# Gated MLP's up projection by Strassen's scheme over pairs of weight tiles

## The chip, the cores and the metric

One Trainium2 chip, one of its cores, one launch. The metric is the time of the program on the device in microseconds (us). The median of 3 runs of the kernel before is 1575.73 us (1575.71 to 1576.24).

The engines of a core have queues of their own and work them off in order: PE multiplies matrices, PEld is its weight load, DVE is the vector engine, ACT the scalar engine, POOL the GpSimd engine, and SP issues the transfers from memory. They wait for each other by semaphores.

## The reference

Two layers of a hybrid encoder, 512 tokens of 1024 columns, all in float32. A layer has attention with a short convolution beside it, merged and projected (`w_o`), then the gated MLP, then a gated embedding. What the change touches is the MLP:

```python
h = rmsnorm(x, g_ffn[i])                     # 512 x 1024
u = dwconv(h @ w_up[i], w_ffn_conv[i])       # 512 x 5632, three taps over the tokens
gate, value = jnp.split(u, 2, axis=-1)       # 2816 each
x = x + (silu(gate) * value) @ w_down[i]
```

(The four lines put the reference's MLP together in short form.)

## The kernel before

Every product is taken at near float32 precision from half-width parts: an operand is split into a high part, which ACT makes by a cast (`hh`, `wh`, `gth`), and a residue, which DVE makes by a subtraction (`hl`, `wl`, `gtl`). A product is then three matmuls, high by high, high by residue and residue by high (`mm3`, lines 88 to 90). Weights come by `weight`: a load of a 128x1024 tile on SP (L80), the cast on ACT (L83), the subtraction on DVE (L84). The ring of raw tiles holds 3, the rings of split tiles 5 each.

The MLP's up projection has 22 pairs of tiles, a gate tile and a value tile of 128 output columns each. A tile is 8 steps over the 1024 inputs, 3 matmuls each, with all 512 tokens as moving columns: 24 matmuls of 512 columns. Its sum lies in PSUM (`ps_mm` for gate tiles, `ps_sc` for value tiles). Then follow the three taps of the convolution (`taps`, L545 on ACT, L546 and L547 on DVE, read from PSUM), Silu of the gate tile (L572, ACT), the gated product (L574, DVE) and the split of the result (`gth`, `gtl`).

The down projection runs in three chunks, after 8, 16 and 22 pairs: for each half of the output columns and each of the four tiles of 128 tokens, `proj` sums the products of a chunk's pairs in PSUM (`ps_tp` in the first two chunks) and `residual` adds the sum to the stream `xs` (L525, DVE).

The MLP starts behind `w_o`, whose result goes through `residual` and `norm` tile of tokens by tile of tokens: Square with its sum on ACT (L117), the reciprocal root on POOL (L98, L99), scaling on DVE (L122, `ht`), transposes on PE (L125, `ps_tp`), split into `hh` and `hl`. While the last two tiles of tokens are normed, the first three up tiles (`NE = 3`, `ew`, `eo`) are multiplied in halves of 256 tokens. In the first half they need only tiles 0 and 1 of the tokens.

The order on each engine comes from a scheduler that places instructions when their inputs are ready and their buffers free; pools of buffers bind it. Where the change says so, PE's order is as written.

## Time and profile before

| | |
|---|---|
| median of 3 runs | 1575.73 us |
| span of the profiled execution | 1574.1 us |
| matmuls and transposes in the trace | 7288 |
| DVE instructions | 1228, 870.4 us busy |
| ACT instructions | 1088, 684.4 us busy |
| POOL instructions | 153, 103.0 us busy |
| transfers of `w_up` | 88 of 512 KB, 3.5 us from issue to landing |
| transfers of `w_down` | 44 of 512 KB, 3.4 us |

How lines are read: a row of the timeline has start, duration, engine, line, operation, output and inputs with their shapes; a bracket gives the idle time ahead of it and what ended it. A row of a group has the count, the busy time and mean duration in ns of one, and the idle time ahead. In the table of windows each engine has its busy time, and PEclk is the share of full clock granted.

### The profile page before, as it was taken

Reading aid. Unit: us, or ns where it says so; the run is one execution under the profiler, and the core shown is the slowest. Engines: PE = TensorE matmul, PEld = TensorE weight load, DVE = VectorE, ACT = ScalarE, POOL = GpSimd, SP = SyncE. Lnnn points to the kernel's source line nnn. Section 1 sums busy time; section 2 is a strip of 40 time slices with the busy share of each in tenths; the row PEclk is TensorE's granted clock in tenths of the full one; section 3 lists DMA queues with packets and bytes.
Section 4 is the critical chain, followed back from the end, with each engine's and each line's share of the span. In section 5 each row is a group of like instructions: output and inputs, shape, how many; then the busy total and the mean of one; then the engine's idle time right before and its main releaser. Section 6 shows DMA issues by size and latency. Waiting matters only on the chain.

```text
span 1574.1 us, 18521 instructions
## 1 busy us (share of the span) xinstructions
PE 1557.1 (99%) x7288; PEld 1280.1 (81%) x7288; DVE 870.4 (55%) x1228; ACT 684.4 (43%) x1088; POOL 103.0 (7%) x153
## 2 busy tenths in 40 slices
PE   7999999999999999999999999999999999999998
PEld 6888888888888888888888888888888888888886
DVE  7787553436544553555477775443565446535543
ACT  5678732325322431334464886222344234324342
POOL 2800000000000000001055000000000000000010
PEclk9999999999999999999999999999999999999999
DMA  6211122323213221323242102232232222232222
GB/s 205 93 55 41 54 94 94 106 69 129 95 61 130 93 95 58 132 96 94 71 133 81 41 28 92 81 107 81 85 118 94 94 94 94 80 107 94 94 68 79
DMA packets 41430, 142.06 MB, mean 90 GB/s; under 512 B 5761, under 2 KB 6273, under 8 KB 41345
## 3 DMA queue, kind: packets, MB, share of 16 engines
q1 hardware_dynamic: 41344, 140.90, 27.2%
q8 instruction: 57, 0.93, 0.2%
q14 instruction: 29, 0.23, 0.0%
HBM read 138.78 MB, written 2.10 MB: 90 GB/s over the span
## 4 chain that ended last, share of the span: by engine, by line
PE 94%; POOL 2%; DVE 2%; ACT 1%; DMA 1%; issue 1%; SPq 0%; DVEq 0%; POOLq 0%; ACTq 0%
PE ps_mm L89 14%; PE ps_mm L88 14%; PE ps_mm L90 14%; PE ps_sc L89 11%; PE ps_sc L88 11%; PE ps_sc L90 11%; PE ps_tp L89 4%; PE ps_tp L88 4%; PE ps_tp L90 4%; PE ps_tp L428 2%; PE ps_tp L125 1%; POOL rs L99 1%; PE ps_av L440 1%; PE ps_av L439 1%; PE ps_tp L394 1%; PE ps_av L88 1%
## 5 line engine op out<-in xcount | busy, mean ns | idle before, releaser
L84 DVE TENSOR_TENSOR wl<-raw,wh 128x1024 fp32r<-128x1024 f32 (+1 forms) x250 | 304.0, 1217 | 325.1 <-ACT wh L83 322.7
L83 ACT CAST wh<-raw 128x1024 fp32r<-128x1024 f32 (+1 forms) x250 | 260.8, 1046 | 425.6 <-PE ps_tp L90 120.3
L88 PE MATMUL ps_mm<-hh,wh 128*128 128x512 f32 (+1 forms) x832 | 326.4, 392 | 0.5 <-DVE ycv L355 0.5
L89 PE MATMUL ps_mm<-hl,wh 128*128 128x512 f32 (+1 forms) x832 | 322.9, 388 | 0.0
L90 PE MATMUL ps_mm<-hh,wl 128*128 128x512 f32 (+1 forms) x832 | 322.5, 388 | 0.0
L90 PEld LDWEIGHTS ps_mm<-hh,wl 128*128 128x128 f32 x832 | 156.6, 188 | 34.7
L88 PEld LDWEIGHTS ps_mm<-hh,wh 128*128 128x128 f32 x832 | 156.7, 188 | 33.2 <-DVE ycv L355 1.0
L89 PEld LDWEIGHTS ps_mm<-hl,wh 128*128 128x128 f32 x832 | 156.9, 189 | 32.5 <-DVE hl L94 0.4
L89 PE MATMUL ps_sc<-hl,wh 128*128 128x512 f32 (+1 forms) x368 | 142.2, 386 | 0.0
L90 PE MATMUL ps_sc<-hh,wl 128*128 128x512 f32 (+1 forms) x368 | 142.2, 386 | 0.0
L88 PE MATMUL ps_sc<-hh,wh 128*128 128x512 f32 (+1 forms) x368 | 142.1, 386 | 0.0
L98 POOL TENSOR_SCALAR ms<-ms 128x1 f32<-128x1 f32 (+2 forms) x40 | 15.8, 394 | 1389.0 <-ACT junk L117 1360.0
L89 PE MATMUL ps_tp<-wl,gth 128*128 128x512 f32 x256 | 100.6, 396 | 0.0
L90 PE MATMUL ps_tp<-wh,gtl 128*128 128x512 f32 x256 | 100.6, 395 | 0.0
L88 PE MATMUL ps_tp<-wh,gth 128*128 128x512 f32 x256 | 99.9, 395 | 0.0
L88 PEld LDWEIGHTS ps_sc<-hh,wh 128*128 128x128 f32 x368 | 69.3, 188 | 15.3
L90 PEld LDWEIGHTS ps_sc<-hh,wl 128*128 128x128 f32 x368 | 69.3, 188 | 15.3
L89 PEld LDWEIGHTS ps_sc<-hl,wh 128*128 128x128 f32 x368 | 69.3, 188 | 15.3
L93 ACT CAST gth<-fa 128x512 fp32r<-128x512 f32 x44 | 27.3, 620 | 120.1 <-DVE fa L574 120.1
L525 DVE TENSOR_TENSOR xs<-xs,ps_tp 128x512 f32<-128x512 f32 x32 | 21.6, 685 | 85.0 <-PE ps_tp L90 85.0
L572 ACT ACTIVATE fa<-fa 128x512 f32<-128x512 f32 x44 | 27.8, 632 | 88.5 <-DVE fa L547 88.5
L88 PEld LDWEIGHTS ps_tp<-wh,gth 128*128 128x128 f32 x256 | 48.1, 188 | 11.6
(242 smaller groups left out, 2671.2 us busy)
## 6 DMA issues: line engine op xcount, KB each, us to landing
raw<-in_w_up_dram SPq DMA_DIRECT2D x88, 512.0 KB, 3.5
raw<-in_w_down_dram SPq DMA_DIRECT2D x44, 512.0 KB, 3.4
raw<-in_w_g_dram SPq DMA_DIRECT2D x32, 512.0 KB, 3.5
raw<-in_w_z_dram SPq DMA_DIRECT2D x24, 512.0 KB, 3.5
raw<-in_w_o_dram SPq DMA_DIRECT2D x16, 512.0 KB, 3.5
raw<-in_w_pg_dram SPq DMA_DIRECT2D x16, 512.0 KB, 4.2
raw<-in_w_au_dram SPq DMA_DIRECT2D x8, 512.0 KB, 3.5
raw<-in_w_cu_dram SPq DMA_DIRECT2D x8, 512.0 KB, 3.5
```

The costliest lines, as they stand in the source:

```text
L83: nc.scalar.copy(h, raw)
L84: nc.vector.tensor_sub(lo, raw, h.bitcast(F32))
L88: nc.tensor.matmul(o, st[0], mv[0], start=start, stop=False)
L89: nc.tensor.matmul(o, st[0], mv[1], start=False, stop=False)
L90: nc.tensor.matmul(o, st[1], mv[0], start=False, stop=stop)
L93: nc.scalar.copy(hi, src)
L98: nc.gpsimd.tensor_scalar_add(ms, ms, EPS)
L99: nc.gpsimd.tensor_tensor(r, ms, negh[:, :n], ALU.pow)
L125: nc.tensor.transpose(tp[:, j * P:(j + 1) * P], ht[:, j * P:(j + 1) * P], ident)
L428: nc.tensor.transpose(tp[:, k * P:(k + 1) * P], pe[:, k * P:(k + 1) * P], ident)
L525: nc.vector.tensor_tensor(xs[:, t, c], xs[:, t, c], o, ALU.add)
L572: nc.scalar.activation(a, a, AF.Silu)
```

## The change

For 20 of the 22 pairs in each layer, the up projection is calculated by the Strassen scheme with Winograd's sums. A pair is a 2 by 2 problem: the inputs (1024) in two halves of 512, the two tiles of the pair as two halves of columns, and the tokens in two halves of 256. In place of 8 products of blocks it has 7, each of 4 steps by 3 matmuls with 256 moving columns: 84 matmuls of 256 columns in place of 48 of 512. The first two pairs (`NS = 2`) are four early tiles in halves of 256 tokens.

What comes with it:
- Sums of the quarters of h, once per layer on DVE (L581 to L586), split into `sh` and `sl`, and one quarter split again into `hh` and `hl`.
- Per pair four subtractions of 128x512 on POOL, in a chain on the raw weight tiles (`pair`, L614 to L617); three splits of 128x1024 and one of 128x512 (`vh`, `vl`) in place of two of 128x1024.
- Per pair three additions of 256 columns on DVE (L633, L647, L650) and four copies on ACT, which put the four quarters of the result into `C`. The taps now read `C`.
- The down projection runs in chunks of 4 pairs (the last of 2), in pieces of 12 matmuls of 512 columns that stand between the products: `residual` runs 48 times per layer in place of 24. The products of two pairs alternate, in an order of PE that is written by hand (`manual_schedule`).
- The pool of weight buffers is opened per layer and closed ahead of the MLP, where another (`wq`, 4 raw and 8 split tiles) is opened. The ring of `gth` and `gtl` holds 8 instead of 16, and the norms behind the MLP take their scratch from `tmp`.

```diff
-CHUNKS = ((0, 8), (8, 16), (16, 22))
+NS = 2
+NQ = 5
+HS = S // 2
...
+    def rawtile(n=1024):
+        wp, nr, nw = wpool[-1]
+        return wp.tile([P, n], F32, tag="raw", name="raw", bufs=nr)
...
+    def load(src, n=1024):
+        raw = rawtile(n)
         nc.sync.dma_start(raw, src)
-        h = wp.tile([P, n], F32R, tag="wh", name="wh")
-        lo = wp.tile([P, n], F32R, tag="wl", name="wl")
+        return raw
+
+    def wsplit(raw, n=1024, tag="w"):
+        wp, nr, nw = wpool[-1]
+        h = wp.tile([P, n], F32R, tag=tag + "h", name=tag + "h", bufs=nw if tag == "w" else 2)
+        lo = wp.tile([P, n], F32R, tag=tag + "l", name=tag + "l", bufs=nw if tag == "w" else 2)
         nc.scalar.copy(h, raw)
         nc.vector.tensor_sub(lo, raw, h.bitcast(F32))
         return h, lo
...
+    def weight(src, n=1024):
+        return wsplit(load(src, n), n)
...
+        wp, close_wp = pool("wp", l)
+        wpool.append((wp, 3, 5))
...
+        wpool.pop()
+        close_wp()
+        wp, close_wp = pool("wq", l)
+        wpool.append((wp, 4, 8))
...
-        KTOT = NJ
-        NE = 3
-        ew = [weight(w_up[l, i]) for i in range(NE)]
-        eo = [psum("sc" if i % 2 else "mm") for i in range(NE)]
+        ew = [weight(w_up[l, i]) for i in range(2 * NS)]
+        eo = [psum("sc" if i % 2 else "mm") for i in range(2 * NS)]
         for hf in range(2):
             c = slice(hf * 256, hf * 256 + 256)
-            for i in range(NE):
+            for i in range(2 * NS):
                 ws(eo[i][:, c], ew[i], hT, KD, P, 0, c)
         g3 = load_gain(l, 2, ff)
-        for j0, j1 in CHUNKS:
...
-            proj((lambda k, c: gt[k // 2][0][:, k % 2, c], lambda k, c: gt[k // 2][1][:, k % 2, c]),
-                 range(j0, j1), w_down[l], after_d, ("mm", "sc") if j1 == NJ else ("tp",))
+        quarter = [(slice(None), slice(2 * r, 2 * r + 2), slice(4 * k, 4 * k + 4), slice(None))
+                   for r in range(2) for k in range(2)]
+        hf = [ff.tile([P, 2, 4, P], F32, tag="gt", name="hf", bufs=8) for q in quarter]
+        V = nc.vector
+        for o, q in zip(hf, quarter):
+            V.tensor_tensor(o, hh[q].bitcast(F32), hl[q].bitcast(F32), ALU.add)
+        h11, h12, h21, h22 = hf
+        V.tensor_tensor(h22, h22, h21, ALU.add)
+        V.tensor_tensor(h21, h21, h11, ALU.subtract)
+        V.tensor_tensor(h11, h22, h11, ALU.subtract)
+        V.tensor_tensor(h12, h12, h11, ALU.subtract)
+        sh, sl = (ff.tile([P, 3, 2, 4, P], F32R, name=n) for n in ("sh", "sl"))
+        for i, src in enumerate((h22, h11, h12)):
+            split(sh[:, i], sl[:, i], src)
+        split(hh[quarter[2]], hl[quarter[2]], h21)
+
+        def quart(r, k0):
+            return lambda k: (hh[:, 2 * r:2 * r + 2, k0 + k, :], hl[:, 2 * r:2 * r + 2, k0 + k, :])
+
+        def summed(i):
+            return lambda k: (sh[:, i, :, k, :], sl[:, i, :, k, :])
+
+        gt = {}
+
+        def gated(j, u):
+            nc.scalar.activation(u[0], u[0], AF.Silu)
+            nc.vector.tensor_tensor(u[1], u[0], u[1], ALU.mult)
+            if j % 2 == 0:
+                gt[j // 2] = (ff.tile([P, 2, S], F32R, tag="gt", name="gth", bufs=8),
+                              ff.tile([P, 2, S], F32R, tag="gt", name="gtl", bufs=8))
+            split(gt[j // 2][0][:, j % 2, :], gt[j // 2][1][:, j % 2, :], u[1])
+
+        def pair(j):
+            r0, r1 = load(w_up[l, 2 * j]), load(w_up[l, 2 * j + 1])
+            b11, b21, b12, b22 = r0[:, :512], r0[:, 512:], r1[:, :512], r1[:, 512:]
+            w0 = wsplit(r0)
+            w22 = wsplit(b22, 512, "v")
+            g = nc.gpsimd
+            g.tensor_tensor(b22, b12, b22, ALU.subtract)
+            g.tensor_tensor(b12, b12, b11, ALU.subtract)
+            g.tensor_tensor(b11, b11, b22, ALU.subtract)
+            g.tensor_tensor(b21, b21, b11, ALU.subtract)
+            yield
+
+            def product(o, w, off, mv, first):
+                for k in range(4):
+                    c = slice(off + k * P, off + k * P + P)
+                    mm3(o, (w[0][:, c], w[1][:, c]), mv(k), first and k == 0, k == 3, not first)
+
+            C = ff.tile([P, 2, S], F32, tag="C", name="C", bufs=2)
+            U = ff.tile([P, HS], F32, tag="U", name="U", bufs=2)
+            y = psum("av")[:, :HS]
+            product(y, w0, 512, quart(0, 4), True)
+            yield
+            x = psum("mm")[:, :HS]
+            product(x, w0, 0, quart(0, 0), True)
+            nc.scalar.copy(U, y)
+            V.tensor_tensor(C[:, 0, :HS], x, U, ALU.add)
+            w1 = wsplit(r1)
+            yield
+            z = psum("sc")[:, :HS]
+            product(z, w1, 0, summed(0), True)
+            w2 = wsplit(r0)
+            yield
+            product(x, w2, 0, summed(1), False)
+            U = ff.tile([P, HS], F32, tag="U", name="U", bufs=2)
+            Z = ff.tile([P, HS], F32, tag="U", name="Z", bufs=2)
+            nc.scalar.copy(U, x)
+            nc.scalar.copy(Z, z)
+            yield
+            product(x, w1, 512, quart(1, 0), False)
+            V.tensor_tensor(C[:, 1, HS:], x, Z, ALU.add)
+            yield
+            product(z, w22, 0, summed(2), False)
+            V.tensor_tensor(C[:, 1, :HS], z, U, ALU.add)
+            yield
+            product(x, w2, 512, quart(1, 4), False)
+            nc.scalar.copy(C[:, 0, HS:], x)
+            gated(j, [taps(2 * j + i, C[:, i, :]) for i in range(2)])
+
+        def down(j0, j1, after, tags):
+            nk = (j1 - j0) // 2
+
+            def tiles(n):
+                return [weight(w_down[l, n * (NJ // 2) + j0 // 2 + k]) for k in range(nk)]
+
+            wt = tiles(0)
+            for n in range(2):
+                for t in range(NT):
+                    yield
+                    tk = slice(t * P, (t + 1) * P)
+                    o = psum(tags[t % len(tags)])
+                    for i in range(2 * nk):
+                        h, lo = gt[j0 // 2 + i // 2]
+                        wh, wl = wt[i // 2]
+                        c = slice((i % 2) * 512, (i % 2) * 512 + 512)
+                        mm3(o, (h[:, i % 2, tk], lo[:, i % 2, tk]), (wh[:, c], wl[:, c]), i == 0, i == 2 * nk - 1)
+                    after(t, n, o)
+                    if n == 0 and t == 2:
+                        nxt = tiles(1)
+                if n == 0:
+                    wt = nxt
+
+        downs = []
+
+        def piece():
+            while downs and next(downs[0], downs) is downs:
+                downs.pop(0)
+
+        def advance(g, n=1):
+            for _ in range(n if g else 0):
+                next(g, None)
+
+        for j in range(NS):
+            gated(j, [taps(2 * j + i, eo[2 * j + i]) for i in range(2)])
+        region = tc.manual_schedule(engines={mybir.EngineType.PE})
+        region.__enter__()
+        old, new = None, pair(NS)
+        advance(new)
+        for q in range(NS, NJ + 1):
+            nxt = pair(q + 1) if q + 1 < NJ else None
+            advance(old)
+            advance(new)
+            piece()
+            advance(old)
+            advance(new, 2)
+            advance(nxt)
+            piece()
+            advance(old, 2)
+            if old and q % 4 == 0:
+                downs.append(down(q - 4, q, residual, ("tp",)))
+            old, new = new, nxt
+        for _ in range(8):
+            piece()
+        region.__exit__(None, None, None)
...
+        for _ in down(4 * NQ, NJ, after_d, ("mm", "sc")):
+            pass
...
-                norm(t, gn, ff)
+                norm(t, gn, None)
```

(Below `-  for j0, j1` the old loop over pairs is left out; it is the one described above.)

Three places in the order. First PE at the start of the MLP in layer 0. Before, from the eighth matmul of the first early tile on (`ps_mm_3316` is its sum; `ht_3223` and `ht_3232` the two halves of token tile 2):

```order
1519 L88 MATMUL ps_mm_3316<-hh_71,wh_3300 128x256
1520 L89 MATMUL ps_mm_3316<-hl_72,wh_3300 128x256
1521 L90 MATMUL ps_mm_3316<-hh_71,wl_3301 128x256
1522 L125 MATMUL ps_tp_3225<-ident_73,ht_3223 128x128 x4
1523 L125 MATMUL ps_tp_3234<-ident_73,ht_3232 128x128 x4
1524 L88 MATMUL ps_mm_3316<-hh_71,wh_3300 128x256
```

Now, from the last matmul of `w_o` (`ps_sc_3241`) on; `ht_3273` and `ht_3282` are token tile 3, `ps_mm_3326` is the first early tile:

```order
1512 L103 MATMUL ps_sc_3241<-wh_3087,me_2096 128x512
1513 L138 MATMUL ps_tp_3225<-ident_70,ht_3223 128x128 x4
1514 L138 MATMUL ps_tp_3234<-ident_70,ht_3232 128x128 x4
1515 L138 MATMUL ps_tp_3275<-ident_70,ht_3273 128x128 x4
1516 L138 MATMUL ps_tp_3284<-ident_70,ht_3282 128x128 x4
1517 L101 MATMUL ps_mm_3326<-hh_68,wh_3304 128x256
```

The transposes of token tiles 2 and 3 moved ahead of every matmul of the MLP; before, those of tile 2 stood 9 matmuls behind its start and those of tile 3 at row 1583, 70 rows behind.

Second, DVE at the same place. Before, weight splits (`wl`) stand between the norm's operations:

```order
357 L122 SCALAR_TENSOR_TENSOR ht_3223<-xs_70,rs1_3220,gbc_2937 128x512
358 L122 SCALAR_TENSOR_TENSOR ht_3232<-xs_70,rs1_3220,gbc_2937 128x512
359 L84 TENSOR_TENSOR wl_3307<-raw_3304,wh_3306 128x1024
360 L84 TENSOR_TENSOR wl_3313<-raw_3310,wh_3312 128x1024
361 L94 TENSOR_TENSOR hl_72<-ps_tp_3184,hh_71 128x512
362 L84 TENSOR_TENSOR wl_3487<-raw_3484,wh_3486 128x1024
363 L525 TENSOR_TENSOR xs_70<-xs_70,ps_sc_3241 128x512
```

Now, behind the scaling of token tile 3; `hf` are the quarter sums, `wl_3305`, `wl_3311`, `wl_3317` and `wl_3323` the four early tiles:

```order
364 L107 TENSOR_TENSOR hl_69<-ps_tp_3275,hh_68 128x512
365 L581 TENSOR_TENSOR hf_3524<-hh_68,hl_69 128x1024
366 L581 TENSOR_TENSOR hf_3525<-hh_68,hl_69 128x1024
367 L581 TENSOR_TENSOR hf_3526<-hh_68,hl_69 128x1024
368 L107 TENSOR_TENSOR hl_69<-ps_tp_3284,hh_68 128x512
369 L94 TENSOR_TENSOR wl_3305<-raw_3302,wh_3304 128x1024
370 L581 TENSOR_TENSOR hf_3527<-hh_68,hl_69 128x1024
371 L94 TENSOR_TENSOR wl_3311<-raw_3308,wh_3310 128x1024
372 L583 TENSOR_TENSOR hf_3527<-hf_3527,hf_3526 128x1024
373 L94 TENSOR_TENSOR wl_3317<-raw_3314,wh_3316 128x1024
374 L94 TENSOR_TENSOR wl_3323<-raw_3320,wh_3322 128x1024
```

The first weight split stands behind the norm of the last token tile and three sums of h.

Third, DVE at the first taps. Before, taps of the early tiles (`ps_mm_3316`, `ps_sc_3317`, `ps_mm_3318`) and a weight split stand in turn, and PE's next products write other sums:

```order
373 L84 TENSOR_TENSOR wl_3601<-raw_3598,wh_3600 128x1024
374 L547 SCALAR_TENSOR_TENSOR fa_3465<-ps_mm_3316,wfc_3296,fa_3465 128x511
375 L546 SCALAR_TENSOR_TENSOR fa_3470<-ps_sc_3317,wfc_3296,fa_3470 128x511
376 L84 TENSOR_TENSOR wl_3637<-raw_3634,wh_3636 128x1024
377 L546 SCALAR_TENSOR_TENSOR fa_3479<-ps_mm_3318,wfc_3296,fa_3479 128x511
```

Now, from the split of the fourth quarter of h on; `C_3590` is the result of pair 2, `ps_mm_3605` its sum x, `raw_3641` and `raw_3737` are tiles of pairs 3 and 4:

```order
393 L107 TENSOR_TENSOR hl_69<-hf_3526,hh_68 128x2x512
394 L565 SCALAR_TENSOR_TENSOR fa_3560<-ps_mm_3328,wfc_3300,fa_3560 128x511
395 L564 SCALAR_TENSOR_TENSOR fa_3564<-ps_sc_3329,wfc_3300,fa_3564 128x511
396 L602 TENSOR_TENSOR fa_3550<-fa_3546,fa_3550 128x512
397 L94 TENSOR_TENSOR wl_3734<-raw_3641,wh_3733 128x1024
398 L94 TENSOR_TENSOR wl_3742<-raw_3737,wh_3741 128x1024
399 L633 TENSOR_TENSOR C_3590<-ps_mm_3605,U_3591 128x256
```

The first C addition of pair 2, which must have read x before the next product is added onto it, stands behind most taps of the early tiles and the weight splits of the next pairs.

More of the change, by code (lines that the diff above doesn't have):

```diff
@@ L63, in encoder_kernel @@
     cp = ctx.enter_context(tc.tile_pool(name="cp", bufs=1))
[L64 removed]
+    wpool = []
     tmp = ctx.enter_context(tc.tile_pool(name="tmp", bufs=2))
@@ L85, in weight, with mm3 @@
         return h, lo
-    def mm3(o, st, mv, start, stop):
-        nc.tensor.matmul(o, st[0], mv[0], start=start, stop=False)
-        nc.tensor.matmul(o, st[0], mv[1], start=False, stop=False)
-        nc.tensor.matmul(o, st[1], mv[0], start=False, stop=stop)
+    def weight(src, n=1024):
+        return wsplit(load(src, n), n)
+    def mm3(o, st, mv, start, stop, more=False):
+        nc.tensor.matmul(o, st[0], mv[0], start=start, stop=False, skip_group_check=more)
+        nc.tensor.matmul(o, st[0], mv[1], start=False, stop=False, skip_group_check=more)
+        nc.tensor.matmul(o, st[1], mv[0], start=False, stop=stop, skip_group_check=more)
     def split(hi, lo, src):
@@ L114, in norm @@
     def norm(t, g, pool):
-        junk = pool.tile([P, D], BF16, tag="junk", name="junk", bufs=1)
+        junk = pool.tile([P, D], BF16, tag="junk", name="junk", bufs=1) if pool else tmp.tile([P, D], BF16, tag="t2", name="junk", bufs=4)
         ms = sm.tile([P, 1], F32, tag="ms", name="ms")
@@ L120, in norm @@
             c = slice(half * 512, half * 512 + 512)
-            ht = pool.tile([P, 512], F32, tag="ht", name="ht", bufs=3)
+            ht = pool.tile([P, 512], F32, tag="ht", name="ht", bufs=3) if pool else tmp.tile([P, 512], F32, tag="t2", name="ht", bufs=4)
             nc.vector.scalar_tensor_tensor(ht, xs[:, t, c], r, g[:, c], ALU.mult, ALU.mult)
@@ L207, in layer @@
         for i in range(2):
-            raw = wp.tile([P, H * DQK], F32, tag="raw", name="raw", bufs=3)
-            nc.sync.dma_start(raw, w_uq[l, i])
+            raw = load(w_uq[l, i], H * DQK)
             w = tuple(lat_p.tile([P, H * DQK], F32R, name=f"wu{i}{n}") for n in "hl")
@@ L558, in layer @@
         g3 = load_gain(l, 2, ff)
-        for j0, j1 in CHUNKS:
-            gt = {}
-            for j in range(j0, j1):
-                av = []
-                for i in (2 * j, 2 * j + 1):
-                    if i < NE:
-                        o = eo[i]
-                    else:
-                        w = weight(w_up[l, i])
-                        o = psum("sc" if i % 2 else "mm")
-                        ws(o, w, hT, KD, P, 0)
-                    a = taps(i, o)
-                    if i % 2 == 0:
-                        nc.scalar.activation(a, a, AF.Silu)
-                    av.append(a)
-                nc.vector.tensor_tensor(av[1], av[0], av[1], ALU.mult)
-                if j % 2 == 0:
-                    gt[j // 2] = (ff.tile([P, 2, S], F32R, tag="gt", name="gth", bufs=16),
-                                  ff.tile([P, 2, S], F32R, tag="gt", name="gtl", bufs=16))
-                split(gt[j // 2][0][:, j % 2, :], gt[j // 2][1][:, j % 2, :], av[1])
-            def after_d(t, n, o, last=(j1 == NJ)):
-                residual(t, n, o)
-                if last and n == 1:
-                    norm(t, g3, ff)
-            proj((lambda k, c: gt[k // 2][0][:, k % 2, c], lambda k, c: gt[k // 2][1][:, k % 2, c]),
-                 range(j0, j1), w_down[l], after_d, ("mm", "sc") if j1 == NJ else ("tp",))
@@ L592, in layer, with after_d @@
+        for _ in range(8):
+            piece()
+        region.__exit__(None, None, None)
+        def after_d(t, n, o):
+            residual(t, n, o)
+            if n == 1:
+                norm(t, g3, None)
+        for _ in down(4 * NQ, NJ, after_d, ("mm", "sc")):
+            pass
+        ph = ff.tile([P, 2, S], F32R, tag="gt", name="ph", bufs=8)
+        pl = ff.tile([P, 2, S], F32R, tag="gt", name="pl", bufs=8)
+        raw = load(pT[l])
         split(ph, pl, raw.rearrange("p (k s) -> p k s", k=2))
-        pw = [ff.tile([P, D], F32, tag="gt", name="pw", bufs=16) for t in range(NT)]
+        pw = [ff.tile([P, D], F32, tag="gt", name="pw", bufs=8) for t in range(NT)]
@@ L618, in layer @@
         close_ff()
+        wpool.pop()
+        close_wp()
     for l in range(L):
```

7 lines of the change are left out of this document (removed).

## The prediction

> **What bounds the kernel now.** I read the page first: span, busy times and the chain that ended last; then the table of windows for one FF stage.
>
> ```profile
> span 1574.1 us, 18521 instructions
> PE 1557.1 (99%) x7288; PEld 1280.1 (81%) x7288; DVE 870.4 (55%) x1228; ACT 684.4 (43%) x1088; POOL 103.0 (7%) x153
> PE 94%; POOL 2%; DVE 2%; ACT 1%; DMA 1%; issue 1%; SPq 0%; DVEq 0%; POOLq 0%; ACTq 0%
> core 0: us, PE busy (x) PEld busy (x) DVE busy (x) ACT busy (x) POOL busy (x), PEclk, DMA share, GB/s
> 395.00:760.00 365.00, 365.00 (x1579) 294.07 (x1578) 188.10 (x223) 126.74 (x164) 4.17 (x8) 1.00 0.29 94
> ```
>
> The span is 1574.1 us, and 1.6 us lie around it: the median of the runs is 1575.73. PE is busy 99% and is 94% of the chain. Inside the FF stage of layer 0 it is busy all 365.00 us at full clock, while DVE has work for 188.10, ACT for 126.74 and POOL for 4.17. So only fewer or shorter matmuls can help, and whatever is added to DVE or POOL is free until it makes PE wait.
>
> **What is gained.** The price of a matmul is the distance between starts, not its printed length, since matmuls are pipelined.
>
> ```profile
> 559.76 0.40 PE L88 MATMUL ps_sc<-hh,wh 128*128 128x512 f32 x1
> 585.53 0.39 PE L90 MATMUL ps_sc<-hh,wl 128*128 128x512 f32 x1
> 372.29 0.28 PE L90 MATMUL ps_sc<-hh,wl 128*128 128x256 f32 x1
> 375.93 0.28 PE L90 MATMUL ps_mm<-hh,wl 128*128 128x256 f32 x1
> 372.29 0.19 PEld L88 LDWEIGHTS ps_sc<-hh,wh 128*128 128x128 f32 x1
> ```
>
> 110 steps of 512 columns take 25.77 us, 0.2343 each; 31 steps of 256 columns take 3.64, 0.1174 each. A weight load lasts 0.19, yet a 256-column stream runs at 0.117: loads overlap and do not bind. A pair cost 48 × 0.2343 = 11.25 us and now costs 84 × 0.1174 = 9.86. That is 1.38 less, and for 20 pairs in each of 2 layers **55.3 us**. The down products keep their number and width.
>
> **The steady lap.** One pair and two down pieces of 12 matmuls are a lap: PE needs 9.86 + 24 × 0.2343 = 15.48 us. There are 17 such laps in a layer (q = 5 to 21), 34 in all. DVE gets three C additions of 256 columns and a second residual addition; POOL, idle here before, gets four subtractions of 128x512.
>
> ```profile
> L84 DVE TENSOR_TENSOR wl<-raw,wh 128x1024 fp32r<-128x1024 f32 x242 | 295.9, 1224 | 324.3 <-ACT wh L83 322.1 <-PE ps_tp L394 0.5
> L547 DVE SCALAR_TENSOR_TENSOR fa<-ps_mm,wfc,fa 128x511 f32<-128x511 f32 x44 | 33.0, 749 | 1.4
> L94 DVE TENSOR_TENSOR gtl<-fa,gth 128x512 fp32r<-128x512 f32 x44 | 30.5, 692 | 28.8 <-ACT gth L93 28.8
> L94 DVE TENSOR_TENSOR lq_l<-ps_tp,lq_h 128x256 fp32r<-128x256 f32 x8 | 3.3, 416 | 0.4 <-ACT lq_h L93 0.4
> L83 ACT CAST wh<-raw 128x1024 fp32r<-128x1024 f32 x242 | 253.7, 1051 | 422.6 <-PE ps_tp L90 120.3 <-PE ps_mm L89 106.8 <-PE ps_sc L89 72.3
> 375.33 1.23 DVE L84 TENSOR_TENSOR wl<-raw,wh 128x1024 fp32r<-128x1024 f32 x1 [4.75 <-ACT wh L83]
> 376.47 0.74 DVE L546 SCALAR_TENSOR_TENSOR fa<-ps_mm,wfc,fa 128x511 f32<-128x511 f32 x1
> 377.13 1.22 DVE L84 TENSOR_TENSOR wl<-raw,wh 128x1024 fp32r<-128x1024 f32 x1
> ```
>
> With these rows DVE's lap is 4 weight splits (three of the pair, one of the down weights on average) 4.90, 4 taps 3.00, five operations of 512 columns (half split, gated product, its split, two residuals) 3.46 and three of 256 columns 1.25: 12.6 us. Queued operations start about 0.08 before the one ahead ends (376.47 against 375.33 + 1.23), which makes it 11.3. ACT has four casts of 1.05 and some smaller work, under 10 us, and does not bind.
>
> For POOL the trace has no 128x512 operation of this kind.
>
> ```profile
> 821.34 0.22 POOL L253 TENSOR_TENSOR kr<-ra,rb 128x16 f32<-128x16 f32 x1
> 82.34 0.46 POOL L253 TENSOR_TENSOR qc<-ra,rb 128x128 f32<-128x128 f32 x1
> L252 POOL TENSOR_TENSOR qc<-ra,rb 128x128 f32<-128x128 f32 x8 | 5.5, 688 | 10.1 <-DVE rb L251 10.1
> ```
>
> From 16 to 128 columns it grows by 0.24 us, 2.1 ns a column, so 512 columns give about 1.27; the bounds are 0.69 (DVE's duration for that shape) and 2.75 (four times the mean of 0.688). I take 1.27, the straight line through undisturbed rows: 5.1 us per lap.
>
> Does POOL slow DVE? These rows say it does.
>
> ```profile
> 78.40 0.69 DVE L332 TENSOR_TENSOR qc<-qc,rs 128x512 f32<-128x512 f32 x1 [2.87 <-POOL rs L99]
> 834.75 0.46 POOL L252 TENSOR_TENSOR qc<-ra,rb 128x128 f32<-128x128 f32 x1
> 834.81 0.94 DVE L332 TENSOR_TENSOR qc<-qc,rs 128x512 f32<-128x512 f32 x1 [0.18 <-POOL rs L99]
> 835.17 0.91 POOL L253 TENSOR_TENSOR qc<-ra,rb 128x128 f32<-128x128 f32 x1
> 819.53 1.23 DVE L84 TENSOR_TENSOR wl<-raw,wh 128x1024 fp32r<-128x1024 f32 x1
> 819.59 1.28 POOL L250 TENSOR_TENSOR ra<-krope,cg 128x32 f32<-128x32 f32 x1 [1.01 <-DVE krope L288]
> ```
>
> The DVE product of 0.69 lasts 0.94 when POOL started 0.06 earlier, and the next POOL operation lasts 0.91 for 0.46; a tiny POOL operation lasts 1.28 beside a weight split. Each seems to wait for the whole of the other. [...] Nothing overlapping, a lap is 11.3 + 5.1 = 16.4 us; with the DVE operations that read PSUM (the C and residual additions, 2.2 queued) hidden under POOL it is 14.2. PE's 15.48 lies between. So a lap loses from 0 to 0.92 us. I take 0.2, because DVE's queue has idle time that takes most POOL operations: 34 × 0.2 = **6.8 us**, with 0 and 31 as bounds. [...]
>
> **The start of each FF stage.** Here the order shows the loss.
>
> ```profile
> 333.25 28.30 SPq L80 DMA_DIRECT2D raw<-in_w_up_dram  x7
> 358.79 0.39 PE L90 MATMUL ps_sc<-wh,me 128*128 128x512 f32 x1
> 359.01 0.28 PE L88 MATMUL ps_mm<-hh,wh 128*128 128x256 f32 x1
> 361.12 0.68 DVE L525 TENSOR_TENSOR xs<-xs,ps_sc 128x512 f32<-128x512 f32 x1
> 362.83 1.05 ACT L117 ACTIVATE junk<-xs 128x1024 bf16<-128x1024 f32 x1
> 364.97 1.41 DVE L122 SCALAR_TENSOR_TENSOR ht<-xs,rs,gbc 128x512 f32<-128x512 f32 x2 [0.79 <-POOL rs L99]
> ```
>
> Before, FF matmuls follow the last w_o matmul without a gap (358.79, 359.01), on weights loaded from 333 on and split ahead; the norm of the last row tile (361.12 to 366.4, over 5 us) is covered. Call 359.0 T. Now all transposes of the norm stand ahead of the first FF matmul in PE's queue, so PE waits for that chain, to about T + 5. Behind it DVE's queue holds two residue splits and three quarter sums, then the first weight split: T + 5 + 2 × 0.6 + 3 × 1.14, and with the casts' waits T + 11.6. The three other weight splits alternate with sums of h, to T + 17. So the four early tiles, 192 matmuls of 0.1174 = 22.5 us, of which few can start ahead of the first split, end near T + 11.6 + 22.1 = T + 33.7 in place of T + 24.4 (22.5 and 1.9 of transposes): **9.3 us** lost. Loads 2 to 4, now issued only after w_o, land before their casts on ACT come up, so they add nothing. Next, pair 2's products y, x and z follow, 12 matmuls each, to T + 37.9; the product added onto x waits until the first C addition (L633) has read x, and this stands on DVE behind the taps of three early tiles and the weight splits of the next pairs, whose casts wait for six POOL operations in series: T + 41.7 to 44.4, so **3.8 to 6.5** more. A product of a later pair (z, whose weight goes through POOL, cast and split) waits about 1.6. Sum 14.7 to 17.4; I take **17 per layer, 34 us**, near the upper end since POOL's chain and DVE's sums lie in the same stretch. With POOL at 0.69 per operation it is 12, with every operation waiting for another over 20.
>
> **The layer boundary.** Opening the weight pool anew per layer lets the w_a loads of layer 1 start only when w_pg's tiles are free.
>
> ```profile
> 781.87 0.33 SPq L80 DMA_DIRECT2D raw<-in_w_a_dram  x1
> raw<-in_w_a_dram SPq DMA_DIRECT2D x8, 416.0 KB, 4.0
> ```
>
> Before, the last of the four loads was issued at 781.87, under w_pg. Now it follows the first split: 4.0 for the load and about 0.9 and 1.0 for cast and split, of which about **5 us** is not covered; bounds 0 and 9.
>
> **Sum.** 55.3 − 34 − 5 − 6.8 = 9.5; 1575.7 − 9.5 = **1566 us** (own time 1574.1 + 1.6).
>
> **The rivals.**
>
> A, slower: DVE and POOL never overlap and DVE becomes the bound, lap 16.4. Then 34 × 0.92 = 31.3 in place of 6.8: about 1591, and each 0.15 us that a POOL operation lasts longer than 1.27 adds 34 × 4 × 0.15 = 20, so 1611 at 1.42. It decides from a mean lap of 15.48 + 16.3/34 = 15.96 on. For it speaks that DVE and POOL together have more than PE's lap of work; against it, that a fifth of DVE's work reads PSUM.
>
> B: the start is mostly hidden, some 6 us per layer, since matmuls that need only the high part of a weight, which ACT delivers earlier, fill the wait, and laps lose nothing: 1575.7 − 55.3 + 12 + 5 = 1537. The long queue of sums ahead of the first weight split speaks against it.
>
> C: 256-column products are bound by weight loads, 84 × 0.19 = 16.0 per pair, 40 × (16.0 − 11.25) = 190 us slower. The spacing of 0.117 all but excludes it. That the change does less than it says is this case too.
>
> D: the clock. After the first 7.63 us of the execution, in which PE waits, matmuls of 416 columns start 0.35 apart, later 0.19.
>
> ```profile
> 9.93 0.55 PE L89 MATMUL ps_mm<-wl,hh 128*128 128x416 f32 x1
> 10.28 0.58 PE L90 MATMUL ps_mm<-wh,hl 128*128 128x416 f32 x1
> 21.47 0.35 PE L88 MATMUL ps_mm<-wh,hh 128*128 128x416 f32 x1
> 21.66 0.35 PE L89 MATMUL ps_mm<-wl,hh 128*128 128x416 f32 x1
> ```
>
> If the wait at the start of FF does this for 4.5 us, half of that is lost, 2.2 per layer: 1570. [...]
>
> **How the numbers follow.** Forecast with its bounds (1556 to 1580) 0.48, A 0.30, B 0.15, D 0.05, C 0.02. The range 1542 to 1602 leaves out half of B, the upper part of A, and C. A measurement of this kernel can tell 0.2%, 3.2 us, from no change. Faster: 0.40 of the forecast, B and 0.03 of D, 0.58. Same: 0.08, 0.06 of A and 0.02 of D, 0.16. Slower: 0.24 of A and C, 0.26.
>
> **What would show it.** Right: laps near 15.7 us in the steady stretch with 256-column starts 0.117 apart; PE idle of about 5 and then 6 us early in each FF stage, released by DVE's wl; PE idle by w_a's split at the boundary. Wrong: laps above 16 with PE waiting for DVE, weight splits of over 1.5 us and POOL operations of over 2 us (A); a start within 6 us of its work (B).

## The result and the profile after

The changed kernel takes **1643.94 us** in the median of 4 runs (1640.36 to 1647.87), the kernel before 1575.99 beside it: a ratio of **1.0431** (95% interval 1.0414 to 1.0449). The forecast was 1566 us: the measured time lies outside the range on the slow side, beyond rival A's 1591 and 1611.

First the page of the changed kernel: span, busy times, the slices of POOL and of PE's granted clock, and the chain.

```profile
span 1643.8 us, 22339 instructions
PE 1542.8 (94%) x8776; PEld 1344.5 (82%) x8776; DVE 1162.6 (71%) x1500; ACT 805.0 (49%) x1336; POOL 364.5 (22%) x313
...
POOL 2700000003343343411045000000034334343110
PEclk9999999998899999999999999999898999999999
...
PE 43%; DVE 17%; issue 8%; ACT 3%; DMA 3%; POOL 1%; DVEq 0%; ACTq 0%; POOLq 0%; SPq 0%
```

PE is idle for 101 us where it was idle for 17, and its share of the chain fell from 94% to 43%; DVE now has 17%. PE's busy time fell by only 14 us, though the matmuls are 55 us shorter by their spacing: in part because some of them ran at a lower clock (0.86 from 350 to 450 us, below). POOL's new work lies in the two FF stages, and the clock is below full where these begin. The table of windows says the same for layer 0 (columns: PE, PEld, DVE, ACT, POOL busy, granted clock, DMA share, GB/s):

```profile
350.00:400.00 50.00, 41.23 (x280) 38.25 (x278) 41.71 (x41) 23.85 (x32) 17.13 (x12) 0.86 0.32 106
400.00:450.00 50.00, 38.07 (x256) 36.41 (x257) 37.98 (x44) 22.69 (x37) 14.02 (x9) 0.86 0.28 85
500.00:550.00 50.00, 45.43 (x316) 41.65 (x315) 44.48 (x47) 25.98 (x40) 19.51 (x12) 1.00 0.33 97
```

Before, PE was busy all through this stage. In the steady laps (last row) it now lacks 4.6 of 50 us, and DVE, which holds it up, is itself idle for 5.5: DVE is not simply full while PE waits for it.

The time by stages, from starts in PE's timeline, last matmul of `w_o` to last down matmul: the FF stage took 373.5 us in each layer and takes 406.7 and 404.7; between the two stages it is 6.5 us longer, behind the second 1.3 shorter. 33.2 + 31.2 + 6.5 − 1.3 = 69.6 us, the difference of the spans.

The groups of DVE and POOL, by form, name the place:

```profile
L564 DVE SCALAR_TENSOR_TENSOR fa<-C,wfc,fa 128x511 f32<-128x511 f32 x80 | 93.9, 1213 | 24.4 <-ACT fa L563 24.4
L565 DVE SCALAR_TENSOR_TENSOR fa<-C,wfc,fa 128x511 f32<-128x511 f32 x80 | 131.1, 1675 | 0.0
L614 POOL TENSOR_TENSOR raw<-raw 128x512 f32<-128x512 f32 x40 | 62.4, 1560 | 427.4 <-DVE vl L94 427.4
L615 POOL TENSOR_TENSOR raw<-raw 128x512 f32<-128x512 f32 x40 | 70.1, 1754 | 2.9
```

The taps, 0.75 us before, last 1.21 and 1.68 in the mean. And all 39 waits of POOL's first subtraction end with the same DVE operation, `vl`, the half split. One lap in the timelines of DVE, POOL, ACT and PE, put together in order of time, shows what that does:

```profile
573.40 0.68 DVE L94 TENSOR_TENSOR vl<-raw,vh 128x512 fp32r<-128x512 f32 x1
574.00 2.44 DVE L564 SCALAR_TENSOR_TENSOR fa<-C,wfc,fa 128x511 f32<-128x511 f32 x2
574.16 1.73 POOL L614 TENSOR_TENSOR raw<-raw 128x512 f32<-128x512 f32 x1 [12.23 <-DVE vl L94]
575.97 1.62 POOL L615 TENSOR_TENSOR raw<-raw 128x512 f32<-128x512 f32 x1
576.36 3.48 DVE L565 SCALAR_TENSOR_TENSOR fa<-C,wfc,fa 128x511 f32<-128x511 f32 x2
577.62 1.05 ACT L93 CAST wh<-raw 128x1024 fp32r<-128x1024 f32 x1 [2.85 <-POOL raw L615]
577.67 1.63 POOL L616 TENSOR_TENSOR raw<-raw 128x512 f32<-128x512 f32 x1
579.37 1.59 POOL L617 TENSOR_TENSOR raw<-raw 128x512 f32<-128x512 f32 x1
579.38 0.28 PE L102 MATMUL ps_sc<-sl,wh 128*128 128x256 f32 x1
579.76 2.28 DVE L94 TENSOR_TENSOR wl<-raw,wh 128x1024 fp32r<-128x1024 f32 x1
582.10 0.38 PE L103 MATMUL ps_sc<-sh,wl 128*128 128x256 f32 x1 [2.43 <-DVE wl L94]
```

`vl` releases POOL, and the four taps stand right behind `vl` on DVE. So the chain on POOL runs beside the taps (144 of the 160 taps of Strassen pairs overlap a POOL subtraction), and the two alternate: four taps take 5.8 us, where four of 0.75, each starting 0.08 before the last one ends, take 2.7. The cast of the second weight is ready at 578.7, but its split stands behind the taps and, itself stretched by POOL's last subtraction, ends at 582.0. PE wanted it at 579.5, one spacing after its last start. That wait comes in about every second lap (the second row: total us, number and longest of these waits):

```profile
POOL raw L614 <- DVE vl L94: 427.4, 39, 19.1
PE ps_sc L103 <- DVE wl L94: 48.0, 20, 4.3
```

### The profile page after: what moved, and what is told of

It is laid out like the page before. It is cut to its first block, busy times and chain, and to the rows that moved or that the text cites. A ratio compares the mean times of both kernels' runs of the same rounds, so it can differ in the third digit from the quotient of the medians.

```text
span 1643.8 us, 22339 instructions
## 1 busy us (share of the span) xinstructions
PE 1542.8 (94%) x8776; PEld 1344.5 (82%) x8776; DVE 1162.6 (71%) x1500; ACT 805.0 (49%) x1336; POOL 364.5 (22%) x313
## 3 DMA queue, kind: packets, MB, share of 16 engines
q1 hardware_dynamic: 41344, 140.90, 27.8%
## 4 chain that ended last, share of the span: by engine, by line
PE 43%; DVE 17%; issue 8%; ACT 3%; DMA 3%; POOL 1%; DVEq 0%; ACTq 0%; POOLq 0%; SPq 0%
PE ps_mm L101 6%; PE ps_mm L103 6%; PE ps_mm L102 6%; DVE fa L565 5%; PE ps_sc L103 5%; DVE fa L564 4%; PE ps_sc L101 4%; PE ps_sc L102 4%; DVE wl L94 4%; DMA raw<-in_w_down_dram 3%; PE ps_tp L103 3%; PE ps_tp L101 2%; PE ps_tp L102 2%; ACT wh L93 1%; DVE xs L539 1%
## 5 line engine op out<-in xcount | busy, mean ns | idle before, releaser
L93 ACT CAST wh<-raw 128x1024 fp32r<-128x1024 f32 (+1 forms) x290 | 297.9, 1045 | 393.3 <-PE ps_mm L102 85.1
L94 DVE TENSOR_TENSOR wl<-raw,wh 128x1024 fp32r<-128x1024 f32 (+1 forms) x290 | 372.9, 1290 | 149.9 <-ACT wh L93 148.4
L101 PE MATMUL ps_mm<-hh,wh 128*128 128x256 f32 (+1 forms) x992 | 337.0, 340 | 4.3 <-ACT wh L93 3.2
L103 PE MATMUL ps_mm<-hh,wl 128*128 128x256 f32 (+1 forms) x992 | 332.5, 335 | 5.8 <-DVE wl L94 5.8
L102 PE MATMUL ps_mm<-hl,wh 128*128 128x256 f32 (+1 forms) x992 | 332.4, 335 | 0.0
L614 POOL TENSOR_TENSOR raw<-raw 128x512 f32<-128x512 f32 x40 | 62.4, 1560 | 427.4 <-DVE vl L94 427.4
L565 DVE SCALAR_TENSOR_TENSOR fa<-C,wfc,fa 128x511 f32<-128x511 f32 x80 | 131.1, 1675 | 0.0
L564 DVE SCALAR_TENSOR_TENSOR fa<-C,wfc,fa 128x511 f32<-128x511 f32 x80 | 93.9, 1213 | 24.4 <-ACT fa L563 24.4
L103 PE MATMUL ps_sc<-sh,wl 128*128 128x256 f32 x160 | 51.9, 324 | 48.0 <-DVE wl L94 48.0
L103 PEld LDWEIGHTS ps_tp<-wh,gtl 128*128 128x128 f32 x320 | 61.5, 192 | 18.1 <-DVE gtl L107 3.3
L102 PEld LDWEIGHTS ps_tp<-wl,gth 128*128 128x128 f32 x320 | 61.7, 193 | 11.4
L615 POOL TENSOR_TENSOR raw<-raw 128x512 f32<-128x512 f32 x40 | 70.1, 1754 | 2.9
L616 POOL TENSOR_TENSOR raw<-raw 128x512 f32<-128x512 f32 x40 | 67.6, 1689 | 10.0 <-issue 3.6
```

What stands on the lines that cost most here:

```text
L93: nc.scalar.copy(h, raw)
L94: nc.vector.tensor_sub(lo, raw, h.bitcast(F32))
L101: nc.tensor.matmul(o, st[0], mv[0], start=start, stop=False, skip_group_check=more)
L102: nc.tensor.matmul(o, st[0], mv[1], start=False, stop=False, skip_group_check=more)
L103: nc.tensor.matmul(o, st[1], mv[0], start=False, stop=stop, skip_group_check=more)
L564: nc.vector.scalar_tensor_tensor(a[:, 1:], o[:, :-1], wfc[:, i, 0:1], a[:, 1:], ALU.mult, ALU.add)
```

## The experiments

Each run is compared with the kernel before on the same chip (1576 us). "Lap" is the mean of 14 steady laps of layer 0, from the starts of the first C addition (L633 in the changed kernel); "C1" is when that addition comes first, from T, the end of `w_o`; "FF" is the stage of layer 0 as above. Kernels with a range or a ratio in the text ran 4 to 7 times and scattered by 1 to 8 us; the others are single runs, and a few us between them mean nothing.

| run | time, us | FF | C1 | lap |
|---|---|---|---|---|
| changed kernel | 1643.94 | 406.7 | T + 47.3 | 17.07 |
| no weight sums | 1560.42 | 364.5 | 41.6 | 15.51 |
| POOL on scratch | 1586.11 | 377.4 | 45.4 | 15.72 |
| sums on DVE | 1571.83 | 370.3 | 41.2 | 15.53 |
| weight pool kept | 1633.83 | 402.0 | 37.5 | 17.47 |
| POOL chain early | 1614.85 | 393.3 | 52.0 | 16.38 |
| half on POOL | 1590.10 | 378.4 | 44.3 | 15.75 |
| sums on DVE and pool kept | 1565.22 | 369.3 | 32.8 | 15.69 |
| and four plain pairs | 1560.60 | 366.0 | 51.0 | 15.45 |
| and first chunk later | 1539.24 | 356.2 | 52.3 | 15.49 |

(The last two have two Strassen pairs fewer per layer, and C1 comes behind four plain pairs.)

**1. No weight sums**

```diff
-            g.tensor_tensor(b22, b12, b22, ALU.subtract)
-            g.tensor_tensor(b12, b12, b11, ALU.subtract)
-            g.tensor_tensor(b11, b11, b22, ALU.subtract)
-            g.tensor_tensor(b21, b21, b11, ALU.subtract)
```

> Leaves out the four POOL subtractions per pair, so the products use the weights unsummed. Theory L (POOL and DVE hold each other up: the chain on POOL is released by the half split vl and so always meets the taps behind it): taps go back to 0.75 us each, the steady lap from 17.07 to about 15.5, the time to about 1585 (34 laps x 1.55 = 53, and some of the start). Theory C (the lap is long because the second and third weights wait for the POOL chain of 6.5 us): the same, 1585. Theory Q (DVE simply has too much queued work in an unlucky order): laps stay above 16.5, above 1620.

1560.42 us in a single run; laps of 15.51, taps of 0.746. The windows show PE busy throughout again:

```profile
500.00:550.00 50.00, 50.00 (x345) 46.29 (x345) 37.70 (x52) 26.30 (x43) 0.00 (x0) 1.00 0.33 103
```

The lap is PE's own 15.48: theory Q falls. The four POOL operations cost 84 us in all, more than L and C had said, and half of it lies at the start of the stages: in layer 0 C1 comes 5.7 us earlier, and the fifth C addition 21 (T + 86.4 in place of T + 107.9).

**2. POOL on a scratch tile**

```diff
-            g.tensor_tensor(b22, b12, b22, ALU.subtract)
-            g.tensor_tensor(b12, b12, b11, ALU.subtract)
-            g.tensor_tensor(b11, b11, b22, ALU.subtract)
-            g.tensor_tensor(b21, b21, b11, ALU.subtract)
+            dm = ff.tile([P, 512], F32, tag="dm", name="dm", bufs=1)
+            g.tensor_tensor(dm, w22[0].bitcast(F32), w22[1].bitcast(F32), ALU.subtract)
+            for i in range(3):
+                g.tensor_tensor(dm, dm, dm, ALU.subtract)
```

> Also leaves the weight sums out, but POOL does four subtractions of 128x512 per pair on a scratch tile, released by vl as the real ones are; no weight waits for them. L: taps stay at about 1.2 and 1.7 us, laps at 16.5 to 17.1, the time at 1620 to 1645. C: taps don't matter, laps near 15.5, about 1590. Q: as in the run without sums, over 1620.

1586.11 us in a single run, and laps of 15.72. The taps are still stretched, if somewhat less (80 us more than 160 taps of 0.746, against 106 in the changed kernel):

```profile
L564 DVE SCALAR_TENSOR_TENSOR fa<-C,wfc,fa 128x511 f32<-128x511 f32 x80 | 111.7, 1433 | 2.6 <-ACT fa L563 2.6
L565 DVE SCALAR_TENSOR_TENSOR fa<-C,wfc,fa 128x511 f32<-128x511 f32 x80 | 87.7, 1132 | 0.0
```

So theory L in its simple form, stretched operations filling DVE's lap, falls: they cost 0.2 us of the lap when no weight waits for POOL. Against the run without sums, POOL's mere presence costs 26 us, nearly all of it at the start of the stages (in layer 0 the FF stage is 12.9 us longer, and the fifth C addition comes 11.5 us later, at T + 97.9); the other 58 came only where the weights depend on it.

**3. The sums on DVE**

```diff
-            g = nc.gpsimd
+            g = nc.vector
```

> The four subtractions move from POOL to DVE, everything is computed. L: taps 0.75 us; DVE's lap is 11.3 + 4 x 0.61 = 13.7 us, under PE's 15.48; laps 15.5 to 16.2, the time 1590 to 1615. C: the chain is shorter (2.4 us) but stands in DVE's queue, so laps fall by half, 1615 to 1630. Q: more work on DVE makes it worse, above 1650.

1571.83 us (7 runs, 1570.56 to 1575.51), ratio to before 0.9974 (0.9963 to 0.9986): faster than L had said. Laps of 15.53. The chain of the second weight is still there, on the busier engine, but nothing on it is stretched:

```profile
565.04 0.69 DVE L94 TENSOR_TENSOR vl<-raw,vh 128x512 fp32r<-128x512 f32 x1
565.77 0.69 DVE L614 TENSOR_TENSOR raw<-raw 128x512 f32<-128x512 f32 x1
566.49 0.69 DVE L615 TENSOR_TENSOR raw<-raw 128x512 f32<-128x512 f32 x1
567.10 0.74 DVE L564 SCALAR_TENSOR_TENSOR fa<-C,wfc,fa 128x511 f32<-128x511 f32 x1
...
570.29 1.22 DVE L94 TENSOR_TENSOR wl<-raw,wh 128x1024 fp32r<-128x1024 f32 x1
```

From the start of `vl` to the end of the second weight's split it is 6.5 us, where the changed kernel took 8.6 (573.40 to 582.04).

**4. The weight pool kept open**

```diff
-        wpool.pop()
-        close_wp()
-        wp, close_wp = pool("wq", l)
-        wpool.append((wp, 4, 8))
+        wxp, close_wx = pool("wx", l)
+        wx.append(wxp)
...
```

Raw tiles and splits then go round rings of 3 + 1 and 5 + 3 in the two pools.

> The weight pool stays open over both layers as in the kernel before and a second one gives the additional buffers (same ring sizes); all else as in the changed kernel. Theory S (the start and the layer boundary are late because the loads of the first weights are issued only after w_o, so that their splits stand behind the norm and the sums of h): the first matmul that needs a residue of an up weight starts within 7 us of the end of w_o in place of 11.9, waits in the first 107 us of FF fall from about 22 to 12 per layer, the boundary gains 5, together 1615 to 1625. Rival N (the norm of the last token tile and the sums of h set the start whatever the loads do): less than 8 us gained, above 1635. Steady laps stay at 17.1 in both.

1633.83 us, ratio 1.0368 (1.0353 to 1.0384): about 10 us less than the changed kernel, half of what theory S said at least, and a little more than the 8 of rival N. FF matmuls follow `w_o` at once, as before (359.01 and 359.24 in PE's timeline), and the part between the two stages falls from 410.8 to 403.6. But in the FF stage only 4.7 us (layer 0) and 2.6 (layer 1) are left, since the wait moved:

```profile
397.31 0.55 PE L111 MATMUL ps_mm<-sh,wh 128*128 128x256 f32 x1 [6.95 <-DVE C L639]
401.31 0.58 PE L112 MATMUL ps_mm<-sl,wh 128*128 128x256 f32 x1 [3.45 <-DVE sl L117]
```

PE reaches pair 2 earlier and there waits for the C addition and for the sums of h.

**5. POOL's chain early**

```diff
-            g.tensor_tensor(b22, b12, b22, ALU.subtract)
+            s22 = ff.tile([P, 512], F32, tag="rs", name="rs", bufs=1)
+            g.tensor_tensor(s22, b12, b22, ALU.subtract)
...
-            g.tensor_tensor(b11, b11, b22, ALU.subtract)
+            g.tensor_tensor(b11, b11, s22, ALU.subtract)
...
-            w1 = wsplit(r1)
+            w1 = wsplit2(b12, s22)
```

(`wsplit2` splits the two halves one by one.)

> POOL does the same four subtractions, everything is computed; the first one writes a tile of its own, so the chain no longer waits for the half split vl, and the second weight's sums are ready about a lap earlier (its split is made in two halves). Theory C (PE waits because the second weight comes out of a chain vl, POOL, POOL, cast, split that starts too late): laps fall from 17.07 to 15.5-15.9, the time to 1585-1605, though taps or other DVE operations still meet POOL operations and are stretched. Theory L (the stretched DVE operations alone fill DVE's lap): laps stay above 16.5, the time above 1620.

1614.85 us in a single run, lap 16.38: between the two. By the starts of the first product of each pair on PE, three laps of four are at 15.51 and the fourth takes 18.4 to 19.8, where a down product waits for the split of a result, which now stands behind the stretched operations:

```profile
PE ps_tp L112 <- DVE gtl L116: 21.0, 8, 2.7
```

So neither C nor L alone holds. A new theory B: PE waits where something it needs soon stands on DVE behind operations that POOL stretches; both the order and the stretching are needed. By "the lock" the next expectation means this stretching as the changed kernel shows it: of the 160 taps that read `C`, 108 lasted 1.75 to 1.79 us, all of them beside a POOL subtraction, and the other 52 lasted 0.74 to 0.75.

**6. Half of the sums on POOL**

```diff
             g.tensor_tensor(b12, b12, b11, ALU.subtract)
-            g.tensor_tensor(b11, b11, b22, ALU.subtract)
-            g.tensor_tensor(b21, b21, b11, ALU.subtract)
+            V.tensor_tensor(b11, b11, b22, ALU.subtract)
+            V.tensor_tensor(b21, b21, b11, ALU.subtract)
```

> POOL keeps the first two subtractions of a pair (those the second weight needs), the other two move to DVE; everything is computed. Theory B (both together: PE waits for the split of the second weight, which comes late because the lock stretches the taps ahead of it and the POOL operations before it): two of the four taps meet POOL, so the split ends about 2 us earlier than in the changed kernel, the wait of 2.3 us in every second lap nearly goes: laps 15.5-16.1, the time 1585-1605. Theory C alone (the length of the chain over POOL counts, stretched taps don't): the chain vl, POOL, POOL, cast is as long as before, laps stay above 16.7, above 1620.

1590.10 us in a single run, lap 15.75. The second weight's chain over POOL is as long as in the changed kernel, 5.3 us from the start of `vl` to the end of the cast; only what is stretched behind it became less, and in one lap (588.39 to 595.53) the split ended 7.1 us after the start of `vl`, where it took 8.6. C alone falls, and B's 1585 to 1605 holds.

**7. Holes in the kernel before**

```diff
-                        o = psum("sc" if i % 2 else "mm")
+                        o = psum("av" if j in HOLES else "sc" if i % 2 else "mm")
                         ws(o, w, hT, KD, P, 0)
                     a = taps(i, o)
+                    if j in HOLES and i % 2 == 0:
+                        junk = t2("fa")
+                        for r in range(HOLES[j]):
+                            nc.vector.tensor_copy(junk, o)
```

with `HOLES = {9: 0, 11: 2, 13: 4, 15: 6}`, and PE's order of pairs 8 to 15 as written.

> The kernel before, everything is computed, with four holes in PE's stream per layer: the two tiles of pairs 9, 11, 13 and 15 share one PSUM buffer, so the second waits for the taps of the first, with 0, 2, 4 and 6 additional reads of it on DVE: holes of about 2.3, 3.5, 4.7 and 6 us. Theory G (a hole of more than some 2.4 us halves the granted clock afterwards for several us): after the longer holes 512-column matmuls start 0.43 to 0.47 apart instead of 0.234 for some us, the time is 1576 + 2 x 16.5 + 5 to 20 for it. Rival W (the slow matmuls in the changed kernel come from what else runs there, POOL or DVE traffic): spacing 0.234 right behind every hole, 1576 + 33 = 1609.

1631.57 us in a single run, above the 1614 to 1629 of G. Counted from when the next matmul was due, which is 0.16 us more than the bracket, PE waited 3.9, 5.1 and 6.5 us in the first three holes of layer 0. The fourth was filled by down products, and behind them PE waited 3.8 us for the split of pair 15's result. Behind each of these four waits matmuls started at half rate, behind the first one after about 1 us. The third hole in PE's timeline, and the windows behind it (PE, PEld, DVE, ACT, POOL busy, granted clock, DMA share, GB/s):

```profile
577.55 0.79 PE L89 MATMUL ps_av<-hh,wh 128*128 128x512 f32 x1 [6.38 <-DVE fa L578]
578.14 0.63 PE L90 MATMUL ps_av<-hl,wh 128*128 128x512 f32 x1
...
581.98 0.62 PE L90 MATMUL ps_av<-hl,wh 128*128 128x512 f32 x1
582.41 0.43 PE L91 MATMUL ps_av<-hh,wl 128*128 128x512 f32 x1
582.68 0.39 PE L89 MATMUL ps_av<-hh,wh 128*128 128x512 f32 x1
```

```profile
577.50:582.50 5.00, 4.95 (x12) 3.89 (x13) 0.00 (x0) 0.00 (x0) 0.00 (x0) 0.50 0.00 0
583.00:600.00 17.00, 17.00 (x74) 13.66 (x73) 8.85 (x11) 6.16 (x8) 0.00 (x0) 1.00 0.19 63
```

DVE and POOL did nothing in those 5 us, and no transfer started in them: W falls, and G is right that the hole itself brings the half rate. The 2.4 us of G stay an estimate: where a limit lies this run can't say, since its shortest such wait was 3.75 us. The four waits, 19.2 us per layer, cost 27.8; the other 8.6 are slow matmuls.

**8. Sums on DVE and the pool kept**: the edits of 3 and 4 together.

> The sums on DVE and the weight pool kept open, both at once, everything is computed. If the two losses are separate: 1571.8 - 10 = 1562 (1557 to 1567), steady laps 15.5, less than 4 us between the end of w_o and the first early products. If the early loads only move the wait further into the start (as the wait of 7 us for the first C addition in the run with the pool kept): 1568 to 1573.

1565.22 us (5 runs), ratio 0.9932 (0.9918 to 0.9945): 6.6 us better than the sums on DVE alone, inside the range for separate losses, but not for its reason: the FF stage gained 1.0 us in layer 0 (369.3 against 370.3) and nothing in layer 1, since the wait at pair 2 came in place of the earlier one. The gain is at the layer boundary, 402.6 against 412.0, where loads start early again. (The stages come from the profiled executions, 1565.32 and 1575.51 us, and the latter was the slowest of its kernel.)

**9. Four plain pairs, with sums of h early or late.** Pairs 2 and 3 in 512-column matmuls, behind them one split of h:

```diff
-NS = 2
+NS = 4
...
+                    w = weight(w_up[l, i])
+                    o = psum("sc" if i % 2 else "mm")
+                    ws(o, w, hT, KD, P, 0)
...
-        split(hh[quarter[2]], hl[quarter[2]], h21)
...
+        split(hh[quarter[2]], hl[quarter[2]], h21)
...
+        downs.append(down(0, 4, residual, ("tp",)))
```

> As the kernel with the sums on DVE and the weight pool kept, and pairs 2 and 3 calculated the old way (512-column matmuls), with only the second split of the quarter of h moved behind them; everything is computed. 2 x 2 x 1.38 = 5.5 us are given up, for cover of the sums of h at the start: PE's waits of about 13 us and slow matmuls of about 4 in the first 100 us of each FF stage fall below 5: 1565 + 5.5 - 24 = 1546 (1542 to 1552). If those waits come from elsewhere than the sums and the first weight chain: 1565 to 1571.

1560.60 us, ratio 0.9905 (0.9889 to 0.9922). The gain expected was four times as large. The early waits did go, but the first down products came to stand ahead of pair 3's result, and PE waited there 3.1 and 0.7 us and ran slowly behind it (the next start after 0.59 us in place of 0.234):

```profile
415.30 0.79 PE L111 MATMUL ps_tp<-wh,gth 128*128 128x512 f32 x1 [3.08 <-ACT gth L116]
417.26 0.80 PE L113 MATMUL ps_tp<-wh,gtl 128*128 128x512 f32 x1 [0.74 <-DVE gtl L117]
```

With all sums of h moved behind the plain pairs:

> The same with all sums of h placed behind the plain pairs in the program. The sums (about 17 us of DVE) then stand directly ahead of the first sum products: a wait of 4 to 8 us per layer at the z product, 8 to 16 us slower than with the sums early.

1564.78 us in a single run: z waited 4.5 and 2.4 us for the sums, but the wait for `gth` then fell away, so it is about 4 us slower and not 8 to 16.

**10. The first chunk's down products one lap later**

Against the kernel of 9 (its first form):

```diff
-        downs.append(down(0, 4, residual, ("tp",)))
...
-            if old and q % 4 == 0:
+            if q % 4 == 0:
```

> As the kernel with four plain pairs, but the down products of the first chunk begin one lap later, so that they no longer wait for the split of pair 3's result (3.3 and 1.1 us in layer 0, with slow matmuls behind) and no later lap is without down products (there z waited 1.9 and 1.9). Everything is computed. If PE's waits are what is left: 6 to 8 us less per layer, 1545 to 1549. If the wait only moves to the next product of that lap: 1556 to 1561.

**1539.24 us** (5 runs, 1539.02 to 1539.7), ratio to before **0.9768** (0.9754 to 0.9781): better than both kernels, and than expected. The waits account for about 6 us per layer, as said (from 10 us to 4 in an FF stage); what came on top is the clock, since the slow matmuls behind the waits went with them (from 4.4 us to 0.6 in layer 0, granted clock of the whole execution 0.993 and 1.000). PE and its clock over the start and the laps:

```profile
span 1537.3 us, 21836 instructions
PE 1511.6 (98%) x8632; PEld 1313.6 (85%) x8632; DVE 1098.6 (71%) x1624; ACT 791.6 (51%) x1312; POOL 101.4 (7%) x153
```

```profile
350.00:400.00 50.00, 50.00 (x332) 45.48 (x331) 42.95 (x53) 27.21 (x38) 1.59 (x4) 1.00 0.28 97
400.00:450.00 50.00, 47.70 (x324) 43.72 (x323) 46.18 (x64) 28.17 (x41) 0.00 (x0) 1.00 0.37 114
500.00:550.00 50.00, 50.00 (x354) 46.68 (x353) 44.47 (x65) 25.29 (x41) 0.00 (x0) 1.00 0.35 106
```

It keeps 36 of the 40 Strassen pairs and has PE waiting hardly anywhere: 36 × 1.38 = 49.7 us to gain, 36.7 of them measured (1575.95 − 1539.24).

## Why the prediction was wrong, step by step

**The gain, 55.3 us: right.** In the runs whose PE does not wait in the laps (1 and 10), a lap takes 15.51 and 15.49, against 15.48 worked out; weight loads did not bind (C), and the change does what it says.

**The steady lap, 0.2 us lost: the step that failed.** It stood on "DVE's queue has idle time that takes most POOL operations". The chain on POOL does not fall into DVE's idle time, since `vl` releases it right ahead of the taps, every lap. The 14 laps of the table lost 1.59 each, and 15.4 of these 22.3 us are z's wait for the split of the second weight. Carried to 34 laps that mean makes 54 us in place of 6.8. The upper bound of 0.92 failed with it, for another reason: it priced DVE's load (11.3 and 5.1 us against 15.48), and the loss is a wait for one operation while DVE has idle time left. A bound on busy time is no bound on a chain. That DVE and POOL operations lengthen each other, and 1.27 us for a 128x512 operation on POOL, were right: beside POOL's chain a tap of 0.75 us took 1.21 and 1.68 in the mean, and a POOL subtraction 1.56 to 1.75; where DVE stood idle beside it, it lasted 1.30 (589.75 us in POOL's timeline). The lower end of the forecast's lap, 14.2, let operations that read PSUM run beside POOL without taking longer, for which it gave no row; in the changed kernel nine taps that read PSUM did so, at 0.73 to 0.75 us. Rival A had the right engine pair with the wrong mechanism, so its price was too low as well: of its signs, laps above 16 with PE waiting for DVE came, but POOL's subtractions did not last over 2 in the mean, and only 22 of 282 weight splits ran beside them for a good part of their time and were stretched, to 2.23. What a lap loses by the stretching did not follow from the sum of busy times.

**The start, 17 us per layer: the second step that failed, by its size.** The first residue matmul came at T + 11.9 (370.92), 11.6 worked out. The first C addition came at T + 47.3, not 41.7 to 44.4, and after it z waited 2.3 and 4.3. Without POOL's sums the FF stage of layer 0 has 364.5, that is 18.6 over its work (373.5 − 27.65). So 17 is about what the start costs without POOL, though the forecast's 17 had POOL's six operations and z's wait for them in it; that it fits run 1 is in part luck, since some 5 us of the 18.6 are slow matmuls, which the forecast had only as rival D. POOL's chain adds some 21 us in layer 0 up to the fifth C addition (T + 107.9 against T + 86.4); with POOL on scratch it is 11.5, so about half comes from what POOL stretches and the other half only where the weights depend on it. Which wait makes up which part of it was not taken apart further. The first of the 17 laps lies in that stretch, so it can't be added to the 54.

**The boundary, 5 us: right in size.** 6.5 us measured, all of it given back when the pool is kept (403.6 between the stages, 404.4 before).

**The clock (rival D): it happened, 2.2 us per layer was too little.** The granted clock was 0.86 from 350 to 450 us. Summing the spacing above 0.117 and 0.234 where nothing waited, about 9 us at the start of layer 0 and 4 in its laps are slow matmuls (7.5 and 4.7 in layer 1).

**The sum.** −55.3, + 37.4 for the starts without POOL, + 82.3 for POOL's sums in both layers (406.7 − 364.5 and 404.7 − 364.6; laps, starts and the clock's part), + 6.5 − 1.3: 69.6 us on the spans, where the forecast had −55.3 + 34 + 6.8 + 5. The 37.4 is what is left when the 55.3 are taken as gained, so it is no separate measurement. POOL's sums, 82.3 us where the forecast had 6.8 in the laps and a part of its 34, make nearly all of the miss.

What stays open: how the 42 us per layer divide between waits and the clock cannot be read exactly, because a slow matmul also delays what DVE waits for.
